# Conditioning rows of a transformer trunk: weight blocks summed on VectorE instead of TensorE

## The chip, the cores and the metric

The kernel runs on one core of a Trainium2 chip. A core has five engines that run side by side, each with its own instruction queue: TensorE (PE, matrix products; its weight loads are listed as PEld), VectorE (DVE), ScalarE (ACT), GpSimd (POOL) and SyncE (SP), whose queue here issues nearly all DMA transfers. They share the on-chip memory SBUF and, but for GpSimd, the accumulator memory PSUM, and wait for each other by semaphores. The metric is device time in microseconds (us); the profile shows one execution.

## The reference

One encoder layer is applied to two sequences, a prompt of 2048 rows and a sample of 256, each row 1024 wide, all in float32. Each sequence has a conditioning vector `c` of 1024 numbers, from which six rows of 1024 are made, once per sequence:

```python
mod = jax.nn.silu(c) @ ada_w + ada_b          # ada_w is 1024 x 6144
sh1, sc1, gt1, sh2, sc2, gt2 = jnp.split(mod, 6, axis=-1)
h = rmsnorm(x, norm_mix) * (1 + sc1) + sh1
x = x + gt1 * hybrid_mixer(h)                 # a Fourier half and a retention half, then w_out
h = rmsnorm(x, norm_mlp) * (1 + sc2) + sh2
x = x + gt2 * (square(relu(h @ w_mlp_in)) @ w_mlp_out)
y = rmsnorm(x, norm_final)
```

The first 2048 columns of `ada_w` (sh1 and sc1) are needed before any row can go through the mixer. The other 4096, the "later conditioning rows" gt1, sh2, sc2 and gt2, are needed from the output projection on. The retention half computes q, k, v and a gate g from h; it needs a state that is summed from the end of the sequence backward, and one that is summed forward.

## The kernel before

Rows are worked in 18 tiles of 128 (16 of the prompt, 2 of the sample). The kernel runs in stages:

- **Start and Fourier sweep** (to about 160 us). Boot loads; the first conditioning rows (`ada0`, lines 391 to 426); normalisation of every tile and its Fourier input. The normalised tile h is stored to DRAM (`hd`).
- **First sweep**, backward (lines 687 to 722; about 160 to 440 us). For each tile h is loaded (`fetch_h`, two tiles ahead) and split into a high part `hhi` (a cast on ScalarE) and a low part `hlo` (a subtraction on VectorE) by `load_h`, one tile ahead. `proj` makes v and k, 24 matmuls of 128x128 by 512 columns each. `rotary` runs on VectorE, k and v go to DRAM, `state_b` sums the backward state. The work of the Fourier half (`jobs`) is spread over the tiles: its transforms, the matrices that mix them, and its stores. Near the end the weights for q and g are loaded and split (`load_w_in`).
- **Second sweep**, forward (lines 837 to 868; about 445 to 780 us). The same `load_h`; `proj` makes q and g. `retention` of the tile before transposes k and q on TensorE, scales q on VectorE (`qx`), makes the scores (`sc`, `sT`), the forward state (`sfn`) and the output (`o`); `ret_norm` normalises that of the tile before. From the sixth tile on `load_w_out` loads and splits a block of the output weights each tile (`raw`, `wohi`, `wolo`).
- **Output projection** with gate gt1, norm of the MLP with sc2 and sh2, and then the **MLP**, which takes most of the time, with gate gt2 at its end.

The later conditioning rows are made in the first sweep. `ada_jobs` holds 16 steps: two halves `bt` (1: gt1 and sh2; 2: sc2 and gt2), eight blocks `k` of 128 weight rows each. A step (lines 700 to 706) loads two 128x1024 blocks of `ada_w` and issues four fp32 matmuls. The stationary operand is `cT[:, k]`, silu(c) in 32 columns of which two are used, one for each sequence; the moving operand is 512 columns of weights. The four products go to the four groups of 32 partitions of one PSUM bank, `m`, where they add up over the eight blocks. `ada_begin` (345) starts the sum with the bias; `ada_end` (357) copies `m` to SBUF, stores the gate rows to DRAM (`gates`), transposes the rest on TensorE and writes it to `aff`, from which the MLP's norm reads.

Buffers are groups of equal tiles with a fixed number (`SLOTS`, line 25): "S" has 13 tiles of 128x1024, and holds weight blocks (`ada`), h, hhi, hlo, kv, the transposed q and k, and `raw`; "H" has 4 of 128x512; "F" has 12 of 128x1024; "PA" and "PB" have 3 PSUM banks each, "PC" has 2, which `m`, `kvb`, `sc` and `o` share. A tile is free for the next use when its last reader is done. The order of instructions on an engine is not that of the source: a scheduler lays the program out before it runs and may put an instruction ahead of earlier ones when its operands are ready sooner. The order is fixed in the program, and each engine runs its own from front to back.

Of the kernel before, what the change touches and what calls it, by code (L numbers as in the profile page):

```python
# [22 lines left out]
H = 4  # L23
# [8 lines left out]
def encoder(ctx: ExitStack, tc: tile.TileContext, a):  # L32
    nc = tc.nc
    act, dve, pool, pe, sp = nc.scalar, nc.vector, nc.gpsimd, nc.tensor, nc.sync

    cp = ctx.enter_context(tc.tile_pool(name="cp", bufs=1))
# [46 lines left out]
    def mm(out, l, r, first, last):  # L83
        pe.matmul(out, l, r, start=first, stop=last)  # L84

    ident = cp.tile([P, P], F32, name="ident")
    zc = cp.tile([P, 8], F32, name="zc")
    mhalf = cp.tile([P, 4], F32, name="mhalf")
    dve.memset(mhalf, -0.5)
    aff = cp.tile([P, 4, 2, KD], F32, name="aff")  # L90

    def rstd_from(ss, n, scale):
# [5 lines left out]
        return r  # L98

    ada_view = a["ada_w"][0].rearrange("(k p) n -> p k n", p=P)  # L100

    def ada_load(bt, k, tag):
        out = []
        for hf in range(2):
            t = t4("ada", tag)
            c0 = bt * 2048 + hf * 1024
            sp.dma_start(out=t, in_=ada_view[:, k, c0:c0 + 1024])
            out.append(t)
        return out

    w_in_v = a["w_in"][0].rearrange("(k p) n -> p k n", p=P)

# [217 lines left out]
    brow = boot[0:12, 0:512]  # L330
# [6 lines left out]
    cT = boot[:, 512:768].rearrange("p (k s) -> p k s", k=KD)  # L337
    dve.memset(cT, 0.0)
    act.activation(cT[:, :, 0:2], rT[:, 0:16].rearrange("p (s k) -> p k s", s=2), AF.Silu)
    gT = cp.tile([P, 2, KD], F32, name="gT")  # L340
    dve.tensor_copy(gT, rT[:, 16:32].rearrange("p (s k) -> p s k", s=2))

    gates = dram([2, 2, D], "gates")

    def ada_begin(bt):
        m = tps("ada", "PC")
        for j in range(4):
            r = bt * 4 + j
            mm(m[32 * j:32 * j + 32, :], ident[0:12, r:r + 1].to_broadcast([12, 32]), brow, True, False)
        return m  # L350

    def ada_step(m, k, tiles):
        for j in range(4):
            mm(m[32 * j:32 * j + 32, :], cT[:, k, :],
               tiles[j // 2][:, (j % 2) * 512:(j % 2) * 512 + 512], False, k == KD - 1)

    def ada_end(bt, m):
        s = t2("adas", "H")
        act.copy(s, m)
        tr = tps("adat", "PC")  # L360
        for i in range(4):
            pe.transpose(tr[:, i * P:(i + 1) * P], s[:, i * P:(i + 1) * P], ident)
        v = tr.rearrange("p (m j s) -> p s j m", m=4, j=4)

        def shift(dst, j0):
            for s_ in range(2):
                dve.tensor_copy(dst[:, s_, :].rearrange("p (j m) -> p j m", j=2), v[:, s_, j0:j0 + 2, :])

        def scale(dst, j0, g):
            for s_ in range(2):  # L370
                dve.scalar_tensor_tensor(out=dst[:, s_, :].rearrange("p (j m) -> p j m", j=2),
                                         in0=v[:, s_, j0:j0 + 2, :], scalar=1.0,
                                         in1=g.rearrange("p (j m) -> p j m", j=2),
                                         op0=ALU.add, op1=ALU.mult)

        def gate(i, j0):
            for j in range(2):
                sp.dma_start(out=gates[i, :, j * 512:(j + 1) * 512],
                             in_=s[32 * (j0 + j):32 * (j0 + j) + 2, :])

        if bt == 1:
            gate(0, 0)
            shift(aff[:, 3], 2)
        else:
            scale(aff[:, 2], 0, gT[:, 1, :])
            gate(1, 2)

    gF = [1.0 - 2.0 ** (-5.0 - h) for h in range(H)]
    gB = [1.0 - 2.0 ** (-5.5 - h) for h in range(H)]
# [298 lines left out]
    for n, t in enumerate(order):  # L688
        hl = nxt
        if n + 2 < NT:  # L690
            fetch_h(order[n + 2])
        if n + 1 < NT:
            nxt = load_h(order[n + 1])
        if pend is not None:
            sb_state = state_b(*pend, None if pend[0] in (17, 15) else sb_state)
            pend = None
        if n >= 1 and jobs:
            for f in jobs.pop(0):
                f()
# [137 lines left out]
    for n, t in enumerate(order2):  # L837
        hl = nxt
        kv = t4("kv", "S")
        sp.dma_start(out=kv, in_=kvd[t])  # L840
# [12 lines left out]
        q, s_b = qs[:, 0:512], qs[:, 512:1024]  # L853
        qr = t2("qr", "H")
        act.copy(qr, pq)
        rotary(qr, t, q)
        if t not in (15, 17):
            sp.dma_start(out=s_b, in_=sbd[t])
        pg = proj(hl, w_g)
        sg = t4("sg", "F")  # L860
        act.activation(sg[:, 0:512], pg, AF.Silu)  # L861
# [48 lines left out]
    gate = None  # L910
# [353 lines left out]
```

## Time and profile before

| | us |
|---|---|
| median of 3 runs (range) | 2429.57 (2426.75 to 2432.01) |
| profiled execution | 2429.74 |
| its span, first to last instruction | 2427.9 |
| TensorE busy in the span | 2349.3 |
| VectorE busy in the span | 1467.7 |
| ScalarE busy in the span | 1011.1 |

In the profile, "out<-in" names the tile that an instruction writes and those that it reads, without their numbers; "x64" is a count. `proj`, `ada`, `dft`, `hlo` are such names. An fp32 matmul such as those of `ada` leaves two records, one of the split kind (fp32r) one. The chain of work that ended last is followed back from the last instruction: at each step to what released it, or to the instruction before it on its engine; only work on this chain sets the time. In a timeline a row gives the start, the length, the engine, the line, the operation and, in brackets, how long the engine stood idle before it and for whom. A row of waits reads: who waited for whom, us in total, how often, the longest. For one instruction of several shapes a tile's view gives the least, median and most ns.

### The profile page before, as it was taken

To read this page: it belongs to the slowest core of one execution; us is meant where nothing else is said; L and a number is where in the kernel's file an instruction comes from. 1 tells how busy PE (TensorE), PEld (TensorE's weight loads), DVE (VectorE), ACT (ScalarE), POOL (GpSimd) and SP (SyncE) were. 2 spreads that over 40 slices of the span, in tenths; PEclk is the share of its full clock that TensorE was granted. 3 is DMA by queue.
4 is the path that set the end of the run, shared out by engine and by line. 5 is a ranking of instruction groups with operands and counts; after the bars stand their busy time and mean duration, and the time that the engine had idled before them with its cause. 6 is when DMAs were issued, how large, how long until landed. Compare 5 with 4: busy or idle time off the path is not lost.

```text
span 2427.9 us, 30947 instructions
## 1 busy us (share of the span) xinstructions
PE 2349.3 (97%) x11985; PEld 2035.6 (84%) x11985; DVE 1467.7 (60%) x2188; ACT 1011.1 (42%) x1684; POOL 111.3 (5%) x191
## 2 busy tenths in 40 slices
PE   7999999999999999999999999998899999999998
PEld 4777887888788888899999999998588788788886
DVE  3674534334434754755785578555845867767887
ACT  4842222223333542555665566554434423323332
POOL 0101000011111000000000000000000000000000
PEclk9999999999999999999999999999799999999999
DMA  7647558323333456443453345433433644645774
GB/s 280 228 170 255 191 178 312 130 83 131 111 100 123 141 170 195 157 130 124 156 185 121 122 158 189 134 122 130 152 104 117 239 165 173 220 162 209 281 265 168
DMA packets 183771, 411.62 MB, mean 170 GB/s; under 512 B 12052, under 2 KB 80436, under 8 KB 176712
## 3 DMA queue, kind: packets, MB, share of 16 engines
q1 hardware_dynamic: 182040, 405.58, 48.2%
q0 software_dynamic: 1584, 4.06, 0.6%
q8 instruction: 94, 1.54, 0.3%
q14 instruction: 53, 0.43, 0.1%
HBM read 274.05 MB, written 135.54 MB: 169 GB/s over the span
## 4 chain that ended last, share of the span: by engine, by line
PE 78%; issue 11%; DVE 5%; DMA 2%; ACT 2%; POOL 1%; SPq 0%; POOLq 0%; DVEq 0%; ACTq 0%
PE mX L963 31%; PE proj L84 17%; PE mZ L963 16%; PE mY L963 8%; PE o L84 1%; PE ada L84 1%; PE dft L84 1%; POOL rr L97 1%; DMA o<-w_mlp_out 1%; DVE hlo L81 1%; PE kvb L84 1%; PE wo L84 1%; DVE t L239 1%; PE tr L747 1%; DMA hr<-hidd 1%
## 5 line engine op out<-in xcount | busy, mean ns | idle before, releaser
L963 PE MATMUL mX<-woT,ho 128*128 128x512 f32 x1296 | 311.7, 391 | 4.7 <-DVE acc L1179 3.5
L80 ACT CAST ho<-hr 128x512 fp32r<-128x512 f32 x252 | 153.9, 622 | 350.2 <-PE mX L963 213.5
L84 PE MATMUL proj<-whi,hlo 128*128 128x512 f32 x720 | 285.1, 397 | 11.1 <-DVE hlo L81 11.1
L84 PE MATMUL proj<-whi,hhi 128*128 128x512 f32 x720 | 287.3, 399 | 5.8 <-ACT sg L861 3.0
L963 PEld LDWEIGHTS mX<-woT,ho 128*128 128x128 f32 x1296 | 244.2, 189 | 57.3 <-DVE acc L1179 4.3
L84 PE MATMUL proj<-wlo,hhi 128*128 128x512 f32 x720 | 283.4, 394 | 0.0
L963 PE MATMUL mX<-opS,wT 128*128 128x384 f32 x1152 | 208.1, 334 | 1.5 <-DVE wT L81 1.5
L963 PEld LDWEIGHTS mX<-opS,wT 128*128 128x128 f32 x1152 | 200.3, 188 | 2.1 <-DVE wT L81 2.1
L81 DVE TENSOR_TENSOR ho<-hr,ho 128x512 fp32r<-128x512 f32 x252 | 170.5, 685 | 34.1 <-ACT ho L80 33.8
L84 PEld LDWEIGHTS proj<-whi,hlo 128*128 128x128 f32 x720 | 135.7, 188 | 47.1 <-DVE hlo L81 18.1
L84 PEld LDWEIGHTS proj<-whi,hhi 128*128 128x128 f32 x720 | 135.9, 189 | 42.7 <-issue 7.5
L84 PEld LDWEIGHTS proj<-wlo,hhi 128*128 128x128 f32 x720 | 135.9, 189 | 34.3 <-issue 8.4
L81 DVE TENSOR_TENSOR wB<-mr,wB 128x1024 fp32r<-128x1024 f32 x72 | 88.0, 1223 | 81.0 <-ACT wB L80 80.9
L963 PE MATMUL mX<-woB,ho 128*128 128x512 f32 x432 | 113.7, 398 | 22.1 <-ACT woB L80 17.9
L81 DVE TENSOR_TENSOR wT<-t,wT 128x1024 fp32r<-128x1024 f32 x72 | 87.8, 1223 | 74.1 <-ACT wT L80 73.7
L1179 DVE TENSOR_TENSOR acc<-mX,acc 128x512 f32<-128x512 f32 x117 | 79.8, 686 | 66.5 <-PE mX L963 60.6
L963 PEld LDWEIGHTS mX<-woB,ho 128*128 128x128 f32 x432 | 82.2, 191 | 42.0 <-ACT woB L80 18.9
L963 PE MATMUL mY<-woB,ho 128*128 128x512 f32 x432 | 114.0, 398 | 2.3 <-ACT woB L80 1.7
L84 PE MATMUL wo<-wohi,mhi 128*128 128x512 f32 x288 | 113.8, 395 | 1.0 <-ACT mhi L80 1.0
L963 PE MATMUL mZ<-woT,ho 128*128 128x512 f32 x432 | 110.8, 394 | 2.2 <-ACT woT L80 2.0
L80 ACT CAST wT<-t 128x1024 fp32r<-128x1024 f32 x72 | 75.3, 1054 | 89.3 <-PE mX L963 56.3
L84 PE MATMUL wo<-wohi,mlo 128*128 128x512 f32 x288 | 112.3, 391 | 0.0
(241 smaller groups left out, 4335.0 us busy)
## 6 DMA issues: line engine op xcount, KB each, us to landing
mr<-w_mlp_in SPq DMA_DIRECT2D x96, 512.0 KB, 3.9
hidd<-hid SPq DMA_DIRECT2D x48, 768.0 KB, 3.4
hr<-hidd SPq DMA_DIRECT2D x27, 1024.0 KB, 6.9
accd<-acc SPq DMA_DIRECT2D x27, 1024.0 KB, 5.3
acc<-accd SPq DMA_DIRECT2D x27, 1024.0 KB, 5.4
ada<-ada_w SPq DMA_DIRECT2D x48, 512.0 KB, 6.9
h<-hd SPq DMA_DIRECT2D x36, 512.0 KB, 4.3
x<-x_prompt SPq DMA_DIRECT2D x32, 512.0 KB, 4.8
```

The costliest lines, as they stand in the source:

```text
L80: act.copy(hi, src)
L81: dve.tensor_tensor(out=lo, in0=src, in1=hi.bitcast(F32), op=ALU.subtract)
L84: pe.matmul(out, l, r, start=first, stop=last)
L97: pool.tensor_tensor(out=r[:, :n], in0=v[:, :n], in1=mhalf[:, :n], op=ALU.pow)
L239: dve.tensor_tensor(out=o, in0=x, in1=y, op=ALU.subtract)
L747: pe.transpose(o[:, hs], src[:, hs], ident)
L963: pe.matmul(out, l, r, start=first and fresh, stop=last, skip_group_check=not fresh)
L1179: dve.tensor_tensor(out=acc[:, b_], in0=o, in1=acc[:, b_], op=ALU.add)
```

## The change

The later conditioning rows are no longer made by matmuls with the weights as moving operand. They are cut into four pieces `pc` of 1024 columns (gt1, sh2, sc2, gt2) with eight blocks `k` each: 32 steps. A step loads one 128x1024 block and, for each of the two sequences, multiplies it on VectorE by one number per partition (`c2[:, k, s]`) and adds it to a sum `acc` of 128x1024; both sums are tiles of group "S" that live for eight steps. After the last block `ada_end` loads the bias again (`br`, group "H"), and for each of four groups (two sequences, two halves of 512 columns) adds two matmuls into the group's 32 partitions of a PSUM bank: the bias, and the sum with a stationary operand of ones, which adds the 128 partitions. Copy, gate stores, transposes and `aff` follow as before, per piece: pieces 0 and 3 store gates, pieces 1 and 2 are transposed.

A step is issued in each tile of the first sweep but its first (17 steps: pieces 0 and 1, and the first block of piece 2), ahead of `proj`, and in the first 15 tiles of the second sweep (the rest), behind the gate's silu and ahead of `load_w_out`. The conditioning in the boot tile, `cT`, and the bias there are thus not needed after the start.

```diff
+    ones = cp.tile([P, 32], F32, name="ones")
+    dve.memset(ones, 1.0)
+    c2 = cp.tile([P, KD, 2], F32, name="c2")
...
+    dve.tensor_copy(c2, cT[:, :, 0:2])
...
-    def ada_begin(bt):
+    def ada_piece(pc, k):
+        w = t4("ada", "S")
+        c0 = 2048 + pc * 1024
+        sp.dma_start(out=w, in_=ada_view[:, k, c0:c0 + 1024])
+        for s_ in range(2):
+            if k == 0:
+                acc_[s_] = t4("adacc", "S")
+                dve.tensor_scalar(out=acc_[s_], in0=w, scalar1=c2[:, k, s_:s_ + 1], scalar2=None, op0=ALU.mult)
+            else:
+                dve.scalar_tensor_tensor(out=acc_[s_], in0=w, scalar=c2[:, k, s_:s_ + 1], in1=acc_[s_],
+                                         op0=ALU.mult, op1=ALU.add)
+        if k == KD - 1:
+            ada_end(pc)
+
+    def ada_end(pc):
+        br = t2("br", "H")
+        sp.dma_start(out=br[0:12, :], in_=a["ada_b"].rearrange("o (r c) -> (o r) c", c=512))
         m = tps("ada", "PC")
-        for j in range(4):
-            r = bt * 4 + j
-            mm(m[32 * j:32 * j + 32, :], ident[0:12, r:r + 1].to_broadcast([12, 32]), brow, True, False)
-        return m
-
-    def ada_step(m, k, tiles):
-        for j in range(4):
-            mm(m[32 * j:32 * j + 32, :], cT[:, k, :],
-               tiles[j // 2][:, (j % 2) * 512:(j % 2) * 512 + 512], False, k == KD - 1)
-
-    def ada_end(bt, m):
+        for g in range(4):
+            s_, hf = divmod(g, 2)
+            r = 4 + 2 * pc + hf
+            o = m[32 * g:32 * g + 32, :]
+            mm(o, ident[0:12, r:r + 1].to_broadcast([12, 32]), br[0:12, :], True, False)
+            mm(o, ones, acc_[s_][:, hf * 512:hf * 512 + 512], False, True)
         s = t2("adas", "H")
         act.copy(s, m)
+        if pc in (0, 3):
+            for g in range(4):
+                s_, hf = divmod(g, 2)
+                sp.dma_start(out=gates[pc // 3, s_:s_ + 1, hf * 512:hf * 512 + 512], in_=s[32 * g:32 * g + 1, :])
+            return
         tr = tps("adat", "PC")
...
-    ada_jobs = []
-    for bt in (1, 2):
-        ada_jobs += [(bt, k) for k in range(KD)]
-    ada_m = {}
+    ada_jobs = [(pc, k) for pc in range(4) for k in range(KD)]
...
-        if n >= 1 and ada_jobs:
-            bt, k = ada_jobs.pop(0)
-            if k == 0:
-                ada_m[bt] = ada_begin(bt)
-            ada_step(ada_m[bt], k, ada_load(bt, k, "S"))
-            if k == KD - 1:
-                ada_end(bt, ada_m[bt])
+        if n >= 1:
+            ada_piece(*ada_jobs.pop(0))
...
         pend = (t, kv, s_b, q, sg)
+        if ada_jobs:
+            ada_piece(*ada_jobs.pop(0))
         if 5 <= n < 13:
             load_w_out(n - 5)
```

More of the change, by code (lines that the diff above doesn't have):

```diff
@@ L100, in encoder @@
     ada_view = a["ada_w"][0].rearrange("(k p) n -> p k n", p=P)
[L102 to L109, printed above, removed]
     w_in_v = a["w_in"][0].rearrange("(k p) n -> p k n", p=P)
@@ L343, in encoder @@
     gates = dram([2, 2, D], "gates")
-    def ada_begin(bt):
-        m = tps("ada", "PC")
-        for j in range(4):
-            r = bt * 4 + j
-            mm(m[32 * j:32 * j + 32, :], ident[0:12, r:r + 1].to_broadcast([12, 32]), brow, True, False)
-        return m
-    def ada_step(m, k, tiles):
-        for j in range(4):
-            mm(m[32 * j:32 * j + 32, :], cT[:, k, :],
-               tiles[j // 2][:, (j % 2) * 512:(j % 2) * 512 + 512], False, k == KD - 1)
-    def ada_end(bt, m):
+    acc_ = [None, None]
+    def ada_piece(pc, k):
[14 more added lines that the diff above has]
+        sp.dma_start(out=br[0:12, :], in_=a["ada_b"].rearrange("o (r c) -> (o r) c", c=512))
+        m = tps("ada", "PC")
+        for g in range(4):
[4 more added lines that the diff above has]
+            mm(o, ones, acc_[s_][:, hf * 512:hf * 512 + 512], False, True)
         s = t2("adas", "H")
         act.copy(s, m)
+        if pc in (0, 3):
[3 more added lines that the diff above has]
+            return
         tr = tps("adat", "PC")
@@ L362, in ada_end @@
             pe.transpose(tr[:, i * P:(i + 1) * P], s[:, i * P:(i + 1) * P], ident)
[L363 to L373, printed above, removed]
-                                         op0=ALU.add, op1=ALU.mult)
[L376 to L386, printed above, removed]
+        v = tr.rearrange("p (m g r) -> p g r m", m=4, g=4)
+        for s_ in range(2):
+            x = v[:, 2 * s_:2 * s_ + 2, 0, :]
+            if pc == 1:
+                dve.tensor_copy(aff[:, 3, s_, :].rearrange("p (j m) -> p j m", j=2), x)
+            else:
+                dve.scalar_tensor_tensor(out=aff[:, 2, s_, :].rearrange("p (j m) -> p j m", j=2), in0=x, scalar=1.0,
+                                         in1=gT[:, 1, :].rearrange("p (j m) -> p j m", j=2),
+                                         op0=ALU.add, op1=ALU.mult)
     gF = [1.0 - 2.0 ** (-5.0 - h) for h in range(H)]
```

## The prediction

> **What bounds the kernel now.** First the page's table of engines, then the busy time by stretches, and for the first sweep (about 160 to 440 us) the time that instructions writing or reading "ada" tiles hold each engine. Columns of the stretches: length, busy us and instructions of each engine, granted clock, DMA share, GB/s.
>
> ```profile
> span 2427.9 us, 30947 instructions
> PE 2349.3 (97%) x11985; PEld 2035.6 (84%) x11985; DVE 1467.7 (60%) x2188; ACT 1011.1 (42%) x1684; POOL 111.3 (5%) x191
> 160.00:440.00 280.00, 280.00 (x1466) 216.50 (x1465) 136.37 (x269) 65.75 (x92) 23.91 (x27) 1.00 0.64 222
> 445.00:530.00 85.00, 85.00 (x455) 72.86 (x454) 28.40 (x51) 20.82 (x52) 7.80 (x10) 1.00 0.31 107
> 530.00:740.00 210.00, 199.09 (x1138) 167.55 (x1137) 91.37 (x181) 67.94 (x176) 27.76 (x33) 1.00 0.33 111
> 160.00:440.00 280.00, 30.45 (x144) 4.26 (x144) 1.18 (x2) 1.00 0.64 222
> ```
>
> TensorE is busy all 280 us of the first sweep, VectorE for 49% of it; 30.45 us of TensorE there are the ada matmuls. In the second sweep TensorE is full until 530 us and then idles 10.9 us in 210. Next I read the chain that ended last, for the first sweep and for the part of the second where TensorE idles, and then TensorE's waits in the second sweep.
>
> ```profile
> by line: PE proj L84 68.8%; PE ada L84 10.2%; PE dft L84 9.3%; PE kvb L84 5.1%; PE pa L84 2.4%; PE pb L84 2.4%; PE fs L84 1.0%; PE pm L84 0.6%; PE adat L362 0.3%
> by line: PE proj L84 57.5%; PE o L84 11.4%; DVE hlo L81 6.6%; DVE sfn L242 4.5%; DVE qx L760 3.8%; ACT sg L861 3.4%; issue 3.3%; ACT qkT L755 3.3%; PE tr L747 2.8%; ACT qkT L757 2.8%; DVE qx L762 0.9%
> PE proj L84 <- DVE hlo L81: 8.4, 11, 1.3
> PE proj L84 <- ACT sg L861: 3.0, 12, 0.5
> ```
>
> In the first sweep the chain is TensorE alone, so what is taken from TensorE there shortens the kernel. In the second, 15.8% of 160 us of chain is VectorE: TensorE waits up to 1.3 us, once in a tile's round, for hlo, the low half of the next row tile's split. There VectorE is a link and not a filler. This is the whole question: the change takes work from the first place and puts VectorE work into both.
>
> **The change, part by part.** *Removed from the first sweep: the 64 weight matmuls and 8 bias matmuls.* The chain counts 10.2% of 280 us = 28.6 us. What a visit costs is seen in TensorE's timeline, (start, length, instruction):
>
> ```profile
> 402.53 0.40 PE L84 MATMUL proj<-whi,hlo 128*128 128x512 f32 x1
> 402.76 0.40 PE L84 MATMUL proj<-whi,hhi 128*128 128x512 f32 x1
> 403.09 1.05 PE L84 MATMUL ada<-ada,boot 128*32 128x512 f32 x4
> 404.07 0.50 PE L84 MATMUL proj<-wlo,hhi 128*128 128x512 f32 x1
> 404.41 0.40 PE L84 MATMUL proj<-whi,hlo 128*128 128x512 f32 x1
> 317.13 1.05 PE L84 MATMUL kvb<-vz,kv 128*128 128x128 f32 x8
> 318.11 1.06 PE L84 MATMUL ada<-boot,ident 12*32 12x512 f32 x8
> 319.10 1.07 PE L84 MATMUL ada<-ada,boot 128*32 128x512 f32 x8
> ```
>
> A visit lasts 0.98 us, for two matmuls (four records) as for four (eight records, 0.99 us): the 32-column groups run side by side. Besides, projection matmuls start 0.23 us apart, but 0.33 us before the visit and 0.34 us after it: some 0.2 us more. 28.6 us are 29 visits of 0.98; the extra is 29 x 0.2 = 5.8 us where a projection stands on both sides, nothing where visits adjoin. I take 5.4, so 34.0 us are removed (bounds 28.6 and 34.4).
>
> *Added: four closings, each of four bias and four ones matmuls.* The bias rows need only a small load and go together (one visit); the ones wait for the two sums, which end one VectorE operation apart, so two visits: 3 x 1.18 = 3.5 us a closing. Bounds: two visits, 2.4 us, and eight one behind the other in written order, 8 x 0.98 = 7.8 us. Two closings lie in the first sweep (7.1 us); two, with the four transposes of one (0.4 us; the chain has 0.3% of 280 for two), in the second: first sweep -34.0 + 7.1 - 0.4 = **-27.3 us**, second **+7.5 us**.
>
> *Added on VectorE: 32 steps of two operations on 128x1024.* Prices: the fp32 two-input operation in hlo, the one-input scaling of x, and two like operations that take 1.22 and 1.46 us:
>
> ```profile
> L81 DVE TENSOR_TENSOR hlo<-h,hhi 128x1024 fp32r<-128x1024 f32 x18 | 22.1, 1230 | 9.8 <-ACT hhi L80 9.8
> L168 DVE TENSOR_SCALAR x<-x,rr x18: 742/752/755, 7.3 to 140.7; 128x1024 f32<-128x1024 f32 x18
> L242 DVE SCALAR_TENSOR_TENSOR zw<-gd,ab x4: 681/682/693, 170.8 to 177.0; 128x512 f32<-128x512 f32 x4
> L81 DVE TENSOR_TENSOR wlo<-raw,whi x20: 1209/1218/2098, 23.9 to 411.7; 128x1024 fp32r<-128x1024 f32 x20
> L81 DVE TENSOR_TENSOR wolo<-raw,wohi x8: 1458/1459/1490, 553.2 to 682.4; 128x1024 fp32r<-128x1024 f32 x8
> ```
>
> A scaled add on 512 columns (0.68 us) costs what a plain two-input operation of that size does, so I give it 1.23 us on 1024; the eight first steps' operations cost 0.75. The total is 56 x 1.23 + 8 x 0.75 = 75 us. Seventeen steps fall into the first sweep: some 39 us beside 136 of 280, behind a full TensorE; I cost them at nothing. If that cover goes (hlo late there too) some of the 27.3 us isn't collected: a rival below. Fifteen steps fall into the second sweep, and there it depends on the place. One tile's round on VectorE, the GpSimd operation in it, and all 16 of that kind (least/median/most ns):
>
> ```profile
> 549.48 0.69 DVE L760 TENSOR_TENSOR qx<-tr,xi 128x512 f32<-128x512 f32 x1 [3.10 <-ACT qkT L757]
> 550.08 0.68 DVE L762 TENSOR_TENSOR qx<-tr,xi 128x512 f32<-128x512 f32 x1
> 550.68 0.87 DVE L242 SCALAR_TENSOR_TENSOR sfn<-sfn,kvf 128x128 f32<-128x128 f32 x4
> 551.47 1.22 DVE L81 TENSOR_TENSOR hlo<-h,hhi 128x1024 fp32r<-128x1024 f32 x1
> 552.61 0.68 DVE L768 TENSOR_TENSOR qkT<-sc,dec 128x512 f32<-128x512 f32 x1
> 553.21 1.46 DVE L81 TENSOR_TENSOR wolo<-raw,wohi 128x1024 fp32r<-128x1024 f32 x1
> 559.84 0.69 DVE L232 TENSOR_TENSOR q<-qr,rope 128x512 f32<-128x512 f32 x1 [5.18 <-PE o L84]
> 563.69 1.14 DVE L810 SCALAR_TENSOR_TENSOR sg<-sg,rr 128x128 f32<-128x128 f32 x4 [1.82 <-POOL rr L97]
> 567.91 0.69 DVE L760 TENSOR_TENSOR qx<-tr,xi 128x512 f32<-128x512 f32 x1 [3.08 <-ACT qkT L757]
> 552.12 1.47 POOL L784 TENSOR_TENSOR vz<-kv,zc 128x512 f32<-128x512 f32 x1 [6.91 <-DMA mixd<-rT]
> L784 POOL TENSOR_TENSOR vz<-kv,zc x16: 1040/1042/1495, 456.4 to 747.6; 128x512 f32<-128x512 f32 x16
> ```
>
> VectorE is free for 5.2 us behind wolo and 3.1 us ahead of qx; both operations, 2.46 us, fit into either gap at no cost. Between 549.5 and 552.7 us they don't: qx, sfn and hlo stand one behind the other, TensorE waits for the last, and each operation put in there adds its whole 1.23 us. So a step costs between 0 and 2.46 us. (Below nothing is excluded: nothing is taken from VectorE in this sweep.) The nearest row is wolo: its block comes through the same queue and it stands behind hlo in all eight of its rounds. But wolo also waits for a ScalarE cast, and the new operations only for their block. When that lands is what counts:
>
> ```profile
> 559.84 0.32 SPq L858 DMA_DIRECT2D q<-sbd  x1
> 560.56 0.33 SPq L226 DMA_DIRECT2D rope<-c_rope  x1
> 560.95 0.42 SPq L735 DMA_DIRECT2D raw<-w_out  x1
> 561.42 0.46 SPq L840 DMA_DIRECT2D kv<-kvd  x1
> 561.93 0.43 SPq L650 DMA_DIRECT2D h<-hd  x1
> ada<-ada_w SPq DMA_DIRECT2D x48, 512.0 KB, 6.9
> ```
>
> Issued with that group at about 561 us and 6.9 us under way, the block lands at 568, at the edge of the chain. I take one operation in the chain in every second step: 15 x 0.61 = **+9.2 us** (0 to 36.9).
>
> Here a rule of the Trainium skill speaks against the change. Wolo and vz run at the same time, and both are long: 1.46 for 1.22, and 1.47 where vz's median is 1.04. The Trainium skill's GPSIMD Engine Reference, section Specifications, says that GpSimd shares its SBUF interfaces with VectorE and contends with operations of two SBUF inputs; the trace agrees. By it, one new operation beside vz in each step would add 15 x 0.24 = 3.6 us; the sum without it stays as it is, since the second operation and the gaps give room.
>
> *Costed at nothing.* The weight loads are the same 32 of 512 KB; 15 move to a sweep with a DMA share of 0.33. The bias loads (0.33 us of issue each, as for rope) and four more gate stores lie in a queue with idle time, and nothing reads the gates before the next stage. Two more ScalarE copies lie beside an engine that is 42% busy. The small copy and the memset at the start lie beside loads; if not, 0.3 us.
>
> **The sum.** The profiled execution took 2429.74 us (1.84 more than its span; the median of the runs is 0.17 lower). -27.3 + 7.5 + 9.2 = -10.6 gives **2419 us**.
>
> **The rivals.** (1) *All hidden*: both operations always fall into the gaps, as wolo does: -19.8, 2410 us. (2) *One operation in the chain in every step*: 15 x 1.23 = 18.5, so -1.3, 2428 us. The 6.9 us landing speaks for it. It also stands for the 13 tiles of group S: two sums and a block are held in it. If the row tiles split ahead are given up for that, TensorE's idling of 10.9 us in 210 begins at 445 instead of 530, 4.4 us; with half the forecast's delay more, 2428 again. (3) *The first sweep doesn't give the time back*, because hlo is late there as soon as TensorE is shorter: half of 27.3 collected gives 2433 us. No wait of TensorE for VectorE in that chain supports it. (4) *Slower: both operations ahead of hlo in every step of the second sweep.* Place: VectorE's order between qx and hlo. Price: 15 x 2.46 = 36.9, so +17.1, 2447 us; it decides from 19.8/15 = 1.32 us a step on. For it speaks that VectorE's chain has no free time there and that a block, once landed, may go ahead of the split of a later tile; against it, wolo's eight rounds.
>
> **How the numbers follow.** Forecast 0.36, all hidden 0.10, one in every step 0.20, not collected 0.06, slower 0.28. About 0.2% (4.9 us) is what a measurement can tell from no change. Faster takes the forecast nearly whole (0.35) and (1): 0.45. Within 0.2%: (2) and most of (3), 0.24. Slower: (4) and the rest, 0.31. The forecast's own range is 2413 to 2424 us (0.2 to 1.0 us a step); the range of all cases, 2409 to 2449 us, reaches from (1) to (4).
>
> **What would show it.** First sweep: from 160 us until the last kv copy some 27 us shorter, TensorE still full, "ada" at about 7 us of it. Second: two short visits, and rounds near 19 us instead of 18.5; the new operations in the gaps means (1), between sfn and hlo means (4), with TensorE's waits for hlo growing from 8.4 us to 30 or more. The forecast is wrong if TensorE idles in the first sweep, or if the closings cost 7 us each because bias and ones alternate.

## The result, and the profile after

The changed kernel took 2459.22 us (median of 4 runs, 2454.23 to 2462.3), the kernel before 2429.57 us beside it (three runs; a fourth took 9022.63 us and is left out): a ratio of 1.0122, with a 95% interval of 1.011 to 1.0134. It is 29.7 us slower; the forecast was 10.6 us faster. The profiled execution took 2462.3 us, 32.6 more than that of before. First the changed kernel's page, its span and engines; then the busy time by stretches, the two sweeps cut at the first and the last copy of `kv` in the first sweep and at the first matmul of the output projection (columns as in the prediction), and the same two stretches of the kernel before.

```profile
span 2460.4 us, 30857 instructions
PE 2372.0 (96%) x11905; PEld 2048.2 (83%) x11905; DVE 1547.2 (63%) x2254; ACT 1012.3 (41%) x1686; POOL 117.7 (5%) x191
```

```profile
165.64:427.44 261.80, 259.80 (x1339) 212.39 (x1338) 170.18 (x295) 64.99 (x93) 27.09 (x27) 1.00 0.63 209
427.44:785.50 358.06, 335.63 (x1736) 267.33 (x1734) 168.74 (x280) 99.07 (x248) 40.99 (x46) 0.95 0.36 121
```

```profile
163.39:441.07 277.68, 277.68 (x1455) 214.59 (x1454) 133.02 (x263) 65.75 (x92) 23.91 (x27) 1.00 0.65 225
441.07:755.40 314.33, 302.00 (x1701) 255.93 (x1699) 128.53 (x249) 96.43 (x245) 37.76 (x46) 1.00 0.33 113
```

TensorE has 80 records fewer (40 fp32 matmuls of two records each: 72 went, 32 came) and is busy 22.7 us longer. The first sweep is 15.9 us shorter, where 27.3 were forecast. The second is 43.7 us longer, where 16.7 were forecast (7.5 for the closings and 9.2 for VectorE), and three things are new in its row: TensorE is idle for 22.4 us of it (358.06 less 335.63; before 12.3), the granted clock is 0.95 instead of 1.00, and TensorE is busy for 33.6 us more (335.63 less 302.00). Of these 33.6, by the same view for single tiles, 22.7 are the matmuls of two closings, 6.6 lie in `o`, whose 368 records took 46.45 us before and 53.02 now, and 3.4 in the projections. The remaining 4.7 us are 2.3 at the start and 2.4 in the output projection and the MLP.

Now the chain that ended last, for the second sweep, and TensorE's waits there (who waited for whom, us, times, the longest):

```profile
by line: PE proj L84 55.8%; PE o L84 11.0%; PE ada L84 6.1%; PE tr L739 4.1%; DVE adacc L353 3.3%; PE wo L84 2.8%; DVE hlo L81 2.5%; issue 1.8%; DVE sfn L236 1.6%; DVE qx L752 1.5%; PE kvf L84 1.4%; PE sc L84 1.4%; ACT qkT L747 1.3%; ACT qk
```

```profile
PE o L84 <- DVE qkT L760: 12.5, 5, 3.8
PE proj L84 <- DVE hlo L81: 5.7, 6, 1.8
```

For the kernel before, the same view had 8.4 us for hlo and, for the masked scores, this row:

```profile
PE o L84 <- DVE qkT L768: 0.6, 1, 0.6
```

So the matmuls of the closings ("ada", 6.1% of 370 us, 22.6 us for two closings) weigh more than VectorE's sums ("adacc", 3.3%, 12.2 us). The sums do delay TensorE, but mostly at the masked scores `qkT`, not at hlo. TensorE's timeline shows why the closings are dear (start, length, instruction, records):

```profile
303.84 1.04 PE L84 MATMUL ada<-br,ident 12*32 12x512 f32 x2
304.81 1.05 PE L84 MATMUL ada<-adacc,ones 128*32 128x512 f32 x2
305.79 1.04 PE L84 MATMUL ada<-br,ident 12*32 12x512 f32 x2
...
310.65 1.05 PE L84 MATMUL ada<-adacc,ones 128*32 128x512 f32 x2
```

Each row is one matmul (two records) on one group of 32 columns. Bias and ones alternate, as the source has them, and each pair adds into the same group; the eight start 0.97 us apart and take 7.8 us. Sharing a group can't be the whole reason: the bias matmul at 305.79 is on another group than the ones matmul ahead of it, and still starts 0.98 us behind it. The old kernel's four matmuls on four different groups ran in 0.99 us together. The closing of the third piece is dearer still (timeline again; a bracket gives the idle time before and its releaser):

```profile
562.43 0.80 PE L84 MATMUL o<-kv,qkT 128*128 128x128 f32 x2 [3.75 <-DVE qkT L760]
...
567.00 1.91 PE L84 MATMUL ada<-br,ident 12*32 12x512 f32 x2
568.84 1.92 PE L84 MATMUL ada<-adacc,ones 128*32 128x512 f32 x2
...
579.90 1.92 PE L84 MATMUL ada<-adacc,ones 128*32 128x512 f32 x2
581.74 0.80 PE L84 MATMUL proj<-whi,hhi 128*128 128x512 f32 x1
...
585.64 0.39 PE L84 MATMUL proj<-whi,hhi 128*128 128x512 f32 x1
```

and the stretches of those microseconds have the granted clock:

```profile
564.00:567.00 3.00, 3.00 (x16) 2.77 (x14) 1.02 (x2) 0.32 (x1) 0.00 (x0) 0.50 0.02 5
578.00:582.00 4.00, 4.00 (x6) 0.62 (x6) 0.00 (x0) 0.15 (x1) 0.00 (x0) 0.50 0.00 0
586.00:588.00 2.00, 2.00 (x11) 1.60 (x10) 0.00 (x0) 0.00 (x0) 0.00 (x0) 1.00 0.00 0
```

TensorE idles 3.75 us for the masked scores, comes back at half clock, and every matmul of the closing takes 1.84 us from start to start: 14.75 us for one closing. The clock is full again only some 3.8 us after the projections have begun. The Trainium skill, TensorE: Matmul & The Clock Gate, Part 1, says that the clock falls to half after an idle window of about 3.4 us and comes back after about 3.4 us of sustained work. The trace agrees on the fall (0.50 behind 3.75 us) and on the return under projections. It doesn't for the closing: 14.75 us of matmuls without a gap, each on a quarter of the columns, left the clock at 0.50, and the 4.6 us of full-width `o` matmuls ahead of them hadn't brought it back either. The closing of the fourth piece stands behind an equal wait and has the full clock:

```profile
738.79 0.55 PE L84 MATMUL o<-kv,qkT 128*128 128x128 f32 x2 [3.75 <-DVE qkT L760]
...
742.85 1.04 PE L84 MATMUL ada<-br,ident 12*32 12x512 f32 x2
743.82 1.04 PE L84 MATMUL ada<-adacc,ones 128*32 128x512 f32 x2
```

```profile
744.00:746.00 2.00, 2.00 (x5) 0.27 (x4) 0.15 (x1) 1.17 (x8) 0.66 (x2) 1.00 0.53 185
```

There the `o` matmuls did bring it back, and the closing took 7.8 us. So the long closing is an event of some closings and not of all.

Last, VectorE around that wait, with the load and the GpSimd operation that bear on it:

```profile
535.29 0.69 DVE L752 TENSOR_TENSOR qx<-tr,xi 128x512 f32<-128x512 f32 x1 [5.75 <-ACT qkT L749]
...
536.49 3.25 DVE L353 SCALAR_TENSOR_TENSOR adacc<-ada,c,adacc 128x1024 f32<-128x1024 f32 x2
539.67 1.21 DVE L81 TENSOR_TENSOR hlo<-h,hhi 128x1024 fp32r<-128x1024 f32 x1
559.71 2.06 DVE L353 SCALAR_TENSOR_TENSOR adacc<-ada,c,adacc 128x1024 f32<-128x1024 f32 x1
561.70 0.68 DVE L760 TENSOR_TENSOR qkT<-sc,dec 128x512 f32<-128x512 f32 x1
527.17 0.43 SPq L347 DMA_DIRECT2D ada<-ada_w  x1
559.65 1.04 POOL L776 TENSOR_TENSOR vz<-kv,zc 128x512 f32<-128x512 f32 x1 [7.46 <-DMA mixd<-rT]
```

The block was issued at 527.17 us, and VectorE idled 5.75 us before qx, from 529.54 to 535.29. The block had landed by 531 us, since no DMA moved anything for the next 3.5 us (and the next was issued at 534.3):

```profile
531.00:534.50 3.50, 3.50 (x23) 3.02 (x22) 0.00 (x0) 0.81 (x2) 0.00 (x0) 1.00 0.00 0
```

Still, both sums stand behind qx and ahead of hlo. In the next tile one stands ahead of the masked scores, beside vz, and takes 2.06 us for a median of 1.277. VectorE runs its instructions in the program's order, so a sum that was laid behind qx doesn't move into the gap. By the same timeline, in six of the fifteen steps both sums stand between qx and hlo, and in six more one of them stands between hlo and the masked scores.

### The profile page after: what moved, and what is told of

The parts are those of the page before. It is cut to its first block, busy times and chain, and to the rows that moved or that the text cites. A ratio compares the mean times of both kernels' runs of the same rounds, so it can differ in the third digit from the quotient of the medians.

```text
span 2460.4 us, 30857 instructions
## 1 busy us (share of the span) xinstructions
PE 2372.0 (96%) x11905; PEld 2048.2 (83%) x11905; DVE 1547.2 (63%) x2254; ACT 1012.3 (41%) x1686; POOL 117.7 (5%) x191
## 4 chain that ended last, share of the span: by engine, by line
PE 76%; issue 11%; DVE 7%; DMA 3%; ACT 1%; POOL 1%; SPq 0%; POOLq 0%; DVEq 0%; ACTq 0%
PE mX L957 30%; PE proj L84 16%; PE mZ L957 15%; PE mY L957 7%; PE ada L84 2%; PE o L84 2%; DMA o<-w_mlp_out 1%; PE dft L84 1%; DMA ada<-ada_w 1%; DVE adacc L353 1%; POOL rr L100 1%; PE wo L84 1%; PE tr L739 1%; DVE t L233 1%; DVE woT L81 1%
```

## The experiments

Four causes were open after this: the order of the matmuls in a closing; VectorE's sums in the second sweep; the tiles of group S that the sums hold; and, seen only in the experiments, the addresses of buffers, since the change puts 192 bytes per partition of new constants (`ones`, `c2`) ahead of groups V and F. All results (each ratio is to the kernel before, run beside it):

| kernel | median us (range, runs) | ratio, 95% |
|---|---|---|
| grouped | 2438.48 (2430.98 to 2442.89, 10) | 1.0036, 1.0024 to 1.0048 |
| no_sums2 | 2444.28 (2434.07 to 2449.49, 7) | 1.0059, 1.0041 to 1.0076 |
| all_first | 2446.63 (2442.45 to 2460.6, 4) | 1.0092, 1.0057 to 1.0127 |
| hold3 | 2441.03 (2440.1 to 2443.02, 4) | 1.0052, 1.0037 to 1.0067 |
| misaligned | 2430.98 (2427.58 to 2432.32, 10) | 1.0008, 0.9999 to 1.0018 |
| aligned | 2453.72 (2447.38 to 2456.32, 4) | 1.0099, 1.0083 to 1.0115 |
| hold3_al | 2443.63 (2443.26 to 2444.26, 4) | 1.0061, 1.0046 to 1.0076 |
| grouped_al | 2421.94 (2417.46 to 2423.05, 6) | 0.9969, 0.9957 to 0.9981 |
| shift128 | 2443.01 (2441.11 to 2444.33, 4) | 1.0059, 1.0045 to 1.0073 |
| hold3_256 | 2427.94 (2424.96 to 2430.16, 10) | 0.9998, 0.9989 to 1.0007 |
| grouped_al_no_sums2 | 2407.54 (2403.91 to 2409.67, 4) | 0.9912, 0.9898 to 0.9926 |
| late | 2409.73 (2406.95 to 2410.67, 5) | 0.992, 0.9906 to 0.9933 |

**grouped: the changed kernel, with the four bias matmuls of a closing ahead of the four of ones.**

```diff
         for g in range(4):
+            r = 4 + 2 * pc + g % 2
+            mm(m[32 * g:32 * g + 32, :], ident[0:12, r:r + 1].to_broadcast([12, 32]), br[0:12, :], True, False)
+        for g in range(4):
             s_, hf = divmod(g, 2)
-            r = 4 + 2 * pc + hf
-            o = m[32 * g:32 * g + 32, :]
-            mm(o, ident[0:12, r:r + 1].to_broadcast([12, 32]), br[0:12, :], True, False)
-            mm(o, ones, acc_[s_][:, hf * 512:hf * 512 + 512], False, True)
+            mm(m[32 * g:32 * g + 32, :], ones, acc_[s_][:, hf * 512:hf * 512 + 512], False, True)
```

> The changed kernel with each closing's four bias matmuls written ahead of its four matmuls of ones. Theory of the closings (bias and ones alternate in one column group, 7.8 us each, and one ran 14.75 us at half clock): a closing takes about 2 us, which gives 23 us, and the stretch at half clock goes, another 7 us: about 2430 us. Theory of VectorE (the sums stand ahead of hlo and of the masked scores in the second sweep): only the TensorE time of the closings goes, 23 us, and the waits stay: 2436 us. If the closings cost nothing on the chain: 2459 us.

It took 2438.48 us, 20.7 less than the changed kernel. Its first sweep is 250.4 us, 27.3 less than before: the forecast's figure for that sweep. The whole time is nearer to the 2436 us of the theory of VectorE than to 2430. The second sweep, at 341.3 us, is still 27.0 longer than before, and the MLP takes 1454.4 us, 10.7 more than before, though nothing in it was touched. So the closings are one cause and not the only one.

**no_sums2: the changed kernel without the scaled adds of blocks 1 to 7 in the second sweep** (28 operations of VectorE; these blocks are left out of the sums, their loads stay).

```diff
-            else:
+            elif not second_[0]:
                 dve.scalar_tensor_tensor(out=acc_[s_], in0=w, scalar=c2[:, k, s_:s_ + 1], in1=acc_[s_],
```

> The changed kernel without the scaled adds of blocks 1 to 7 in the second sweep (28 VectorE operations); loads, both sum tiles and closings stay. Theory of VectorE: the second sweep loses its waits for hlo and the masked scores, some 21 us of its 44 us of growth, and with them the half clock of one closing, 7 us: 2431 to 2438 us. Theory of the 13 tiles of group S: the sums still hold two of them, so most of the growth stays: 2450 us or more.

2444.28 us, 14.9 less than the changed kernel and between the two expectations. But the seven runs lie between 2434.07 and 2449.49 at one and the same mean granted clock of 0.988 to 0.990, so by itself it gives the size only roughly; it was taken again on a steadier base below.

**all_first: two steps per tile in the first sweep, none in the second.**

```diff
         if n >= 1:
-            ada_piece(*ada_jobs.pop(0))
+            for _ in range(min(2, len(ada_jobs))):
+                ada_piece(*ada_jobs.pop(0))
```

> The changed kernel with two steps per tile in the first sweep, so that all 32 lie there and none in the second. Theory of VectorE: the second sweep is as long as before (314 us from the last kv copy to the first output matmul), and the first sweep pays four closings of 7.8 us for the 34 us removed: 2426 to 2432 us, as before the change. If VectorE, now with 75 us more in 280, is late in the first sweep too: 2440 us or more.

2446.63 us. In the first sweep (276.8 us) TensorE waits 1.7 us and none of it for VectorE, so VectorE isn't late there; its third closing took 11.9 us, at half clock in part. The second sweep, now without any step, is still 325.9 us, 11.6 more than before: seven of the eight matmuls of the last closing ran from 442.0 to 449.4 us, which is in it, and its projection matmuls start 0.233 us apart instead of 0.228. This run speaks against VectorE as the only cause, but closings and addresses are mixed in it; all sums in the first sweep with grouped closings and padding was not run.

**hold3: the kernel before, with three tiles of group S held through 15 tiles of the second sweep.**

```diff
+    hsum = cp.tile([P, 4], F32, name="hsum")
...
+        if n == 0:
+            hold = [t4("hold", "S") for _ in range(3)]
+            for x in hold:
+                dve.tensor_copy(x[:, 0:4], sg[:, 0:4])
+        if n == 14:
+            for x in hold:
+                dve.tensor_tensor(out=hsum, in0=x[:, 0:4], in1=sg[:, 0:4], op=ALU.add)
```

> The kernel before, with three tiles of group S taken and held through the first 15 tiles of the second sweep (three tiny copies in, three tiny adds out). Theory of group S: the second sweep grows by 10 to 20 us: 2440 to 2450 us. Theory of VectorE: at most the earlier start of TensorE's idling, 0 to 4 us: 2430 to 2434 us.

2441.03 us, 12.2 more than before: it looked as if the held tiles were dear. But of the 11.4 us between the profiled spans, 4.2 lie in the second sweep and 7.5 in the MLP, where none of these tiles is held any more. In parts of the MLP, 50 us held 285 matmuls instead of 290, at a granted clock of 1.00 in both. What lasts so long is a position: `hsum` takes 16 bytes per partition (more, if the allocator rounds up), and the tiles allocated behind it on that side of SBUF move up.

**misaligned and aligned: 64 bytes of constants, unused, added to the kernel before, and the same 64 bytes added to the changed kernel.** Group V (in the second sweep the weights of q), group F (among others the weights of g) and later the MLP's left operands lie behind the constants. By the constants' sizes they start 192 bytes later than before in the changed kernel, 64 later in misaligned and 256 later in aligned. The expectations below speak of multiples of 64 and 128; no view shows the addresses themselves, so in what follows only these shifts are given.

```diff
+    even = cp.tile([P, 16], F32, name="even")
+    dve.memset(even, 0.0)
```

> The kernel before with one constant tile of 64 bytes per partition more, so that groups V and F and the MLP's left operands start at an odd multiple of 64 bytes where they started at a multiple of 128. Theory of the addresses (in every changed kernel so far, and in none of before, projections of the second sweep start 0.233 us apart instead of 0.228): the second sweep grows by 864 x 5.5 ns = 4.7 us, the MLP by up to 10 us: 2433 to 2443 us. Otherwise, that the spacing comes from what those kernels do: 2429 us.

> The changed kernel with 64 bytes per partition more, so that those tiles start at a multiple of 128 bytes again. Theory of the addresses: the spacing of projections in the second sweep is 0.228 us as before the change, 4.7 us less there and 3 us or more in the MLP: 2448 to 2452 us. Otherwise 2459 us.

Misaligned took 2430.98 us, no change: not every shift costs, and the expected 2433 to 2443 were wrong. Aligned took 2453.72, 5.5 less than the changed kernel. The intervals of those two ratios just overlap, so the size is rough; what is clear is the pace of the second sweep's projections, 0.228 us again where the changed kernel had 0.233. One start that is 64 bytes further does nothing to the old kernel, and something to the new one.

**hold3_al, hold3_256 and shift128: which shift, and does holding cost anything?** The first two are hold3 with a constant of 128 and of 256 bytes; shift128 is the kernel before with 128 unused bytes and nothing else.

```diff
-    hsum = cp.tile([P, 4], F32, name="hsum")
+    hsum = cp.tile([P, 32], F32, name="hsum")
```

> The kernel before with three tiles of group S held through 15 tiles of the second sweep, now with the constants padded to a multiple of 128 bytes. Theory of the addresses: the 12 us of the same kernel without the padding were the addresses alone; the second sweep keeps its 314 us and the whole is 2429 to 2431 us, so group S costs nothing. Theory of group S: it stays at 2436 us or more.

```diff
-    hsum = cp.tile([P, 4], F32, name="hsum")
+    hsum = cp.tile([P, 64], F32, name="hsum")
```

> The kernel before with three tiles of group S held, with constants padded so that the later tiles start at an odd multiple of 128 bytes as before. Theory of the addresses: 2429 to 2432 us, second sweep 314 to 316 us: three tiles less cost nothing that can be measured. Theory of group S: 2436 us or more.

```diff
+    even = cp.tile([P, 32], F32, name="even")
+    dve.memset(even, 0.0)
```

> The kernel before with 128 bytes per partition of unused constants more, nothing else; groups V and F and the MLP's left operands then start at an even multiple of 128 bytes, as in the padded kernel with held tiles, and no longer at an odd one. Theory of the addresses: projections of the second sweep start 0.233 us apart and the MLP's first half does 286 matmuls in 50 us for 290; 2440 to 2443 us with no change in any instruction's order. Theory of group S (the held tiles cost the 12 to 15 us): 2429 us.

hold3_al took 2443.63 us, where the theory of the addresses had 2429 to 2431: a multiple of 128 bytes isn't what counts. hold3_256 took 2427.94: with 256 bytes, three held tiles cost nothing (ratio 0.9998). And shift128, which holds no tile, took 2443.01, with the instructions of TensorE, VectorE and ScalarE in the order of the kernel before. So the 12 us of hold3 were addresses, wholly. The projection in the second sweep, in the timeline of the kernel before and then of shift128 (same columns as above):

```profile
500.54 0.39 PE L84 MATMUL proj<-whi,hhi 128*128 128x512 f32 x1
...
501.22 0.39 PE L84 MATMUL proj<-whi,hhi 128*128 128x512 f32 x1
```

```profile
500.64 0.39 PE L84 MATMUL proj<-whi,hhi 128*128 128x512 f32 x1
...
501.33 0.40 PE L84 MATMUL proj<-whi,hhi 128*128 128x512 f32 x1
```

These are three intervals each. The starts are 0.227 us apart in the first and 0.232 in the second (means over 470 to 505 us). For the MLP, one group of its matmuls (least, median, most ns) and 50 us of it, first of the kernel before:

```profile
L963 PE MATMUL mX<-opS,wT x1152: 333/334/446, 997.5 to 1679.0; 128*128 128x384 f32 x192
```

```profile
1000.00:1050.00 50.00, 50.00 (x290) 50.00 (x289) 30.84 (x32) 29.46 (x37) 0.00 (x0) 1.00 0.41 132
```

then of shift128:

```profile
L965 PE MATMUL mX<-opS,wT x1152: 336/337/447, 1002.4 to 1693.2; 128*128 128x384 f32 x192
```

```profile
1000.00:1050.00 50.00, 50.00 (x286) 50.00 (x285) 31.38 (x34) 25.67 (x33) 0.00 (x0) 1.00 0.36 116
```

The median matmul of this group is some 1% longer, with TensorE full and the clock at 1.00.

**grouped_al: grouped closings and the 64 bytes.** The edits of grouped and aligned together.

> The changed kernel with grouped closings and with the padding. If closings and addresses add up: 2438.5 - 4.7 - 3 to 10 in the MLP = 2424 to 2431 us, with what is left of the second sweep's growth (waits for hlo and the masked scores, and half clock behind them, some 20 us) against the first sweep's gain of 27. If the addresses matter only in the kernel before: 2438 us.

2421.94 us, faster than the kernel before (0.9969) and than the 2424 to 2431 expected. The first sweep is 250.7 us (27.0 less than before), the second 330.3 (16.0 more), and the MLP 1445.7. Its first closing in TensorE's timeline has two visits, as the forecast had it:

```profile
302.12 1.06 PE L84 MATMUL ada<-br,ident 12*32 12x512 f32 x8
303.11 1.06 PE L84 MATMUL ada<-adacc,ones 128*32 128x512 f32 x8
304.11 0.50 PE L84 MATMUL dft<-tab,zh 128*128 128x256 f32 x2
```

**grouped_al_no_sums2: the same, again without the 28 scaled adds of blocks 1 to 7 in the second sweep** (left out of the sums as in no_sums2).

> The changed kernel with grouped closings and padding, without the scaled adds of blocks 1 to 7 in the second sweep. Theory of VectorE: of the second sweep's 330 us some 10 to 12 go (its two closings, 4 us, and the transposes stay): 2410 to 2412 us, with TensorE's waits for masked scores near nothing. If the waits come from the sum tiles or from the loads: 2420 us.

2407.54 us, 14.4 less: that is what the adds cost in the second sweep, 1.03 us for each of the 14 steps. The second sweep with the adds (grouped_al) and without them:

```profile
414.71:745.03 330.32, 307.60 (x1737) 260.50 (x1735) 167.19 (x281) 98.94 (x248) 41.48 (x46) 0.99 0.39 132
413.05:730.09 317.04, 304.06 (x1736) 257.43 (x1735) 131.54 (x253) 98.58 (x247) 37.81 (x46) 1.00 0.40 138
```

Of the 13.3 us between them TensorE idles 9.7 less and is busy 3.5 less, with the clock at 1.00 instead of 0.99: waits, and half clock behind them. Without the adds that sweep is 2.8 us longer than before, and TensorE still waits 4.8 us for the masked scores.

**late: the same adds at another place.** Each step of the second sweep first writes its two scalars by a tiny operation that also reads the rotated q (times 0), so that the adds can't stand ahead of the rotation; the scalars go into the tile that was padding.

```diff
-    def ada_piece(pc, k):
+    def ada_piece(pc, k, after=None):
...
+        cs = c2[:, k, :]
+        if after is not None:
+            cs = even[:, 2 * k:2 * k + 2]
+            dve.scalar_tensor_tensor(out=cs, in0=after[:, 0:2], scalar=0.0, in1=c2[:, k, :], op0=ALU.mult, op1=ALU.add)
...
-            ada_piece(*ada_jobs.pop(0))
+            ada_piece(*ada_jobs.pop(0), after=q)
```

> The changed kernel with grouped closings and padding, where each step's two VectorE operations in the second sweep depend on the rotated q of their tile (their scalars are written by a tiny operation that reads it), so that they stand in the gap between the rotation and the scaling by the gate, behind the masked scores. Theory of VectorE's place: the same 75 us of VectorE work then costs next to nothing, TensorE's waits for the masked scores fall from 12.6 us to under 2: 2410 to 2415 us. If the amount of VectorE work costs, and not its place: 2422 us.

2409.73 us, 0.992 of the kernel before (0.9906 to 0.9933): the fastest version that does the whole computation, 49.5 us below the changed kernel and faster than both. Of the 14.4 us that the adds cost it gets 12.2 back, with the same VectorE work. In VectorE's timeline:

```profile
548.29 0.69 DVE L228 TENSOR_TENSOR q<-q,rt 128x512 f32<-128x512 f32 x1
549.02 0.16 DVE L352 SCALAR_TENSOR_TENSOR even<-q,c 128x2 f32<-128x2 f32 x1
549.22 2.48 DVE L358 SCALAR_TENSOR_TENSOR adacc<-ada,even,adacc 128x1024 f32<-128x1024 f32 x2
552.60 1.14 DVE L807 SCALAR_TENSOR_TENSOR sg<-sg,rr 128x128 f32<-128x128 f32 x4 [0.90 <-POOL rr L101]
```

and TensorE's waits in that sweep, first of grouped_al, then of late:

```profile
PE o L84 <- DVE qkT L762: 12.6, 5, 3.8
```

```profile
PE tr L744 <- DVE sg L807: 4.7, 1, 4.7
PE o L84 <- DVE qkT L765: 4.1, 3, 1.8
```

The adds now stand behind the rotation and ahead of the gate's scaling `sg`, where VectorE still waits 0.90 us for GpSimd. The wait for the masked scores falls from 12.6 to 4.1 us: not under 2, as expected, but to less than the 4.8 us without the adds. One new wait, for `sg`, takes 4.7. The tie moves what hangs on the sums with them (the ones of the third closing start 6.7 us behind its bias there), so it is the place of the whole step that differs.

## Why the prediction was wrong, by its own steps

*The closings: wrong, and the largest part.* The step that failed reads "the bias rows need only a small load and go together (one visit) ... so two visits: 3 x 1.18 = 3.5 us a closing". It took for granted that the scheduler would collect the four bias matmuls. They ran in the order of the source: 4 x 7.8 = 31.2 us of matmuls instead of 14, and one of the four took 7.0 more. The bound of 7.8 us was on record and the alternation was named as what would make the forecast wrong, but no chance went to it: no rival carried it, and the range's upper end came from VectorE alone. With the order written out (grouped_al), the first sweep gives 27.0 us for a forecast of 27.3. That agreement is in part luck. Grouped, the two closings there took 2 x 2.0 us, not 2 x 3.5, and TensorE waited 2.3 us for VectorE (250.74 less 248.42), where the "nothing" for its 17 steps allowed none and the kernel before had none. The two errors nearly cancel; the removal's price of 34.0 us stands to within some 1 us.

*The half clock: not foreseen.* One closing fell behind an idle stretch and ran at 0.50, 14.75 us instead of 7.8, and slowed what followed for another 3.8; the `o` matmuls behind the three long waits ran at half clock too. Its size can't be had from one trace: the changed kernel's runs at a mean clock of 0.985 or 0.986 took 2454 and 2457 us, those at 0.982 took 2461 and 2462, and in aligned's profile (2447.38 us, clock 0.985) the same closing took 8.1. An estimate from these times is 5 to 8 us, in some executions.

*VectorE in the second sweep: the mechanism was right, its place in part, its size too small.* Forecast 0.61 us a step, 9.2 in all; measured 14.4, or 1.03 a step. The forecast's bounds of 0 and 36.9 held it. The reason was that the sums may stand in the chain between qx and the next split; they did, and also ahead of the masked scores, which the prediction didn't name. What it argued from, the moment at which the block lands, wasn't what decided: in the round shown the block had landed, VectorE idled, and the order laid down beforehand put the sums behind qx. Late shows it: same loads, same work, another place, 12.2 us. Its price for GpSimd's share was also low: it took 0.24 us for an operation beside vz, and one such sum took 2.06 us for a median of 1.277, 0.78 more. What rival (4) had as its price, both operations in the chain in every step, 36.9 us, was not reached, though its place was: six of the fifteen steps have both between qx and hlo. Its sign, looked for in hlo, was not seen there: TensorE's waits for hlo fell from 8.4 to 5.7. The result lies on its side for other reasons.

*The tiles of group S: right to call small.* Three held tiles cost nothing by hold3_256.

*The start: the step that failed in silence.* "The small copy and the memset at the start lie beside loads; if not, 0.3 us." What counted was not their time but their bytes. The 192 bytes moved groups V and F, and padding them to 256 saved 5.5 us in the changed kernel and 16.5 in grouped. The pace of the second sweep's 864 projection matmuls accounts for some 4.7 us of either (864 x 5.5 ns).

*The sum.* The measured steps from the result to the forecast: 2459.22, less 5.5 (padding) is 2453.72; less 31.8 (closings grouped, with what they brought on) is 2421.94; the forecast was 2419. The 31.8 are more than the 23.2 us (4 x 5.8) that eight matmuls cost beyond two visits. The half clock, which lasts longer with a long closing in it, is in the rest; how much of the rest it is stays open. Padding saves three times as much once the closings are grouped, and in the profiles the difference lies in the MLP: 1446.6 us in the changed kernel and 1447.2 in aligned, but 1454.4 in grouped and 1445.7 in grouped_al. The changed kernel and grouped have the same addresses, so why their MLPs differ is open. Grouped's ten runs lie 11.9 us apart, the six of grouped_al 5.6, which would fit a pace that differs between executions; with one trace of each that isn't shown. That the last number comes near the forecast is partly luck: VectorE cost 5 us more than forecast, and the second sweep's closings with all else there only 2.8 instead of 7.5.

## What to carry to other kernels

Where matmuls use groups of 32 columns, write those of one kind together, over all groups (all firsts, then all seconds): here four of one kind took 0.99 us together, and with two kinds alternating each took 0.97 alone. Don't count on the scheduler to collect them. Whether the shared group or the change of kind makes them wait, no run separates; at 305.79 a matmul on another group waited too. When work is moved to an engine with free time, say by a dependency at which gap it is to stand: in the program's order, free time a few microseconds earlier was worth nothing here. And after any change, look at a stage that the change doesn't touch: if it is 1% slower at full clock, look at what moved in memory, and pad.

## What the runs showed of the hardware that was not expected

*Start addresses and TensorE's pace.* The kernels sort by how many bytes their constants push up groups V and F and the MLP's left operands. The counts are of matmul records in stretches of 50 us of the MLP's first half (1100 to 1650 us) in which TensorE is busy throughout, at a clock of 1.00:

| shift, bytes | kernels | projections of the second sweep, us apart | MLP, records in 50 us |
|---|---|---|---|
| 0 or 256 | before; hold3_256, aligned, grouped_al, grouped_al_no_sums2, late | 0.227 to 0.228 | 290 or 291 |
| 64 | misaligned | 0.229 | 290 |
| 128 | shift128, hold3_al | 0.232 to 0.233 | 286 or 287 |
| 16 | hold3 | 0.233 | 285 or 290 |
| 192 | changed, grouped, no_sums2, all_first | 0.233 | 285 to 291 |

128 unused bytes cost 14.6 us of 2428.4 (shift128), most of it in the MLP (9.8 us, all in its first half: 715.5 us before, 726.3 now). The first sweep and the output projection didn't change (0.228 and 0.227 us): their operands lie in groups that didn't move. At 16 and 192 bytes the MLP keeps no one pace: in the changed kernel the stretches from 1100 to 1450 us had 290 or 291 records and those at 1500 and 1600 had 285, while grouped, at the same addresses, had 285 to 288 and no_sums2 288 to 290. So the shift alone doesn't settle it.

Why is open, but the runs narrow it. In the stages that slow down only the moving operand moved (the weights in a projection, the left operands in the MLP); the stationary one lies in groups that stayed. In the MLP's second half both operands lie in the part that moved, and nothing changed there: 728.2 us before and 727.2 in shift128. That would fit a rule about the distance between two operands that are read at once, and not one about the moving operand's start alone; no run moves a stationary operand by itself, so it isn't shown.

*Narrow matmuls and the clock.* In the changed kernel's third closing, matmuls that each use one group of 32 columns kept the clock at 0.50 for 14.75 us, and it came back within some 3.8 us of full-width projections. The fourth closing, behind the same wait of 3.75 us, began at 1.00 and stayed at 1.00 through its 7.8 us. A stage of narrow matmuls right behind an idle stretch can therefore be paid twice; of two such closings in one trace, one was.

*GpSimd beside VectorE.* The scaled add of the changed kernel by its tile (least/median/most ns), and the 28 of the second sweep as a group (busy us, mean ns):

```profile
L353 DVE SCALAR_TENSOR_TENSOR adacc<-ada,c,adacc x56: 1268/1277/2061, 184.3 to 738.7; 128x1024 f32<-128x1024 f32 x56
```

```profile
L353 DVE SCALAR_TENSOR_TENSOR adacc<-ada,c,adacc 128x1024 f32<-128x1024 f32 x28 | 41.7, 1511 | 0.8 <-DMA ada<-ada_w 0.8
```

and the same 28 in late:

```profile
L358 DVE SCALAR_TENSOR_TENSOR adacc<-ada,even,adacc 128x1024 f32<-128x1024 f32 x28 | 35.5, 1310 | 0.5
```

The long ones stand beside vz, and at the place that late gives them the mean falls from 1.51 to 1.31 us. The Trainium skill, GPSIMD Engine Reference, Specifications, has the rule that the two contend on operations with two SBUF inputs; the trace agrees, and the price here was up to 0.78 us for a scaled add. In late the adds are short and GpSimd pays instead: its small operation `rr`, beside which they now stand, took 1.01 us in the second sweep of grouped_al and 1.83 in late (x15 | busy us, mean ns):

```profile
L102 POOL TENSOR_TENSOR rr<-rv,mhalf 128x4 f32<-128x4 f32 x15 | 15.1, 1009 | 1.3 <-POOL rv L99 0.2
L101 POOL TENSOR_TENSOR rr<-rv,mhalf 128x4 f32<-128x4 f32 x15 | 27.5, 1832 | 1.3
```

The gate's scaling `sg` waits for `rr`.
